# Issuing the sum-of-squares matmul behind the seventh contraction tile of a first phase

## The chip, the core and the metric

The kernel runs on one NeuronCore of a Trainium2 chip. The core has a matrix engine (PE, or TensorE), a vector engine (DVE), a scalar engine (ACT), GpSimd (POOL) and DMA queues; each engine works off its own list of instructions in the order in which they were put there, and waits on semaphores for what it needs from the others. The metric is the device time of one execution in microseconds (us).

## What is computed

A decoder trunk of four layers on one sequence of 256 tokens, model width 1024. Each layer is a macaron: a half-step SwiGLU feed-forward network (FFN), a token mixer (differential attention in layers 0 and 3, RWKV-7 in layer 1, sliding-window attention in layer 2), another half-step FFN. Each of these twelve sub-layers first normalises and modulates its input:

```
h = modulate(rms_norm(x, norm_g[i, 0]), sh1, sc1)      # x*rsqrt(mean(x*x)+eps)*g, then *(1+scale)+shift
x = x + 0.5 * g1 * swiglu(h, ffn_w_in[i, 0], ffn_w_out[i, 0])
...
def swiglu(h, w_in, w_out):
    gate, up = jnp.split(h @ w_in, 2, axis=-1)
    return (jax.nn.silu(gate) * up) @ w_out
```

## The kernel before, in words

The model width lies on the 128 partitions, in eight tiles x[0] to x[7] of 128x256 (tokens on the free axis). An fp32 product is made of three fp32r matmuls (`mm3`, lines 287 to 289): every operand is split in a high part hi and a low part lo, and hi·hi, hi·lo and lo·hi are summed. Weights are streamed from memory and split on chip as they come: hi on ACT (L269), lo on DVE (L271, 128x512, four to a slab). DVE also makes the adaLN vectors of the next sub-layers in halves of 128x1024 (`ada`, L350).

A sub-layer's **first phase** is made so that PE need not wait for the normalisation. While the sub-layer before ends, DVE adds each finished output tile to x (L589); then x·(g·(1+scale)), not yet divided by the root mean square, is split into `xh` (`pre`: hi on ACT, lo on DVE, L501). The factor 1/rms is one number per token, so it can be multiplied into the products afterwards: `unraw` (L547 to 554) does that on DVE (L553) on the way out of PSUM, with a shift term that ACT copies (`ub`, L552).

`first_units` (L530) issues the products of the first two or three weight units on `xh`: for each of the eight contraction tiles xh(0) to xh(7) nine matmuls (three output banks by `mm3`), then a fourth bank, then two more per further unit. Somewhere in between it calls `make`, which is `make_h` (L505). This does, in this order:

- `rstd` (L474): the matmul of the sum of squares, three fp32 instructions at L478, of the ones matrix with `ssum` (the squares of the first six tiles, summed up on POOL, L463) and with the last two squares `sq` (ACT, L455), into PSUM bank psc;
- the reciprocal root on DVE (`_rsqrt`): transposition of psc to `rsqt` (L410), ten small 128x8 operations (L419 to L435), transposition back to `rsq` (L441);
- for each of the eight tiles the scaled input: `xr` = x·a·rsq on DVE (L522), the high part of `h` on ACT (L524), the low part on DVE (L525).

The matmuls behind the first phase use `h`. In an FFN these are the up products of the second pair into psd, in the attention mixers products into psb. Their first `mm3` needs the high part of h(0), its second the low part.

This form of first phase stands at ten of the twelve sub-layers' starts. They are called B1 to B10 here, by the time of their sum-of-squares matmul in the profiled run: B1 219.4 us (into differential attention), B2 353.9 (out of it into an FFN), B3 548.5 (FFN into FFN), B4 1062.9 (RWKV into FFN), B5 1257.6 (FFN into FFN), B6 1451.6 (into sliding-window attention), B7 1545.5 (out of it into an FFN), B8 1739.6 (FFN into FFN), B9 1934.9 (into differential attention), B10 2071.0 (out of it into the last FFN). The program's very first FFN and RWKV use other code.

The order of instructions on each engine is not written out by hand. A scheduler fixes it when the kernel is built, from the dependences, the order in which the code issues the work, and its own costs; so a matmul that is issued later can change the order on DVE and ACT as well. At run time each engine keeps to its list.

Of the kernel before, what the change touches and what calls it, by code (L numbers as in the profile page):

```python
# [228 lines left out]
class Trunk:  # L229
# [300 lines left out]
    def first_units(self, w, make, tags):  # L530

        raw = bool(self.xh)
        hs = None if raw else make()
        banks = [self.ps(t) for t in tags for _ in range(2)]
        src, n = (self.xh, T + 2) if raw else (hs, T)
        self.xh = None
        order = [(k, (0, 1, 2)) for k in range(ND)] + [(k, (3,)) for k in range(ND)]
        order += [(k, (f,)) for f in range(4, 2 * len(w)) for k in range(ND)]
        for i, (k, fs) in enumerate(order):
            if raw and i == 4:  # L540
                hs = make()
            for f in fs:
                self.project(w[f // 2], 2, src, [banks[f // 2 * 2][:, :n], banks[f // 2 * 2 + 1][:, :n]], ks=(k,),
                             fs=(f % 2,), own=True)
        return banks, raw, hs
# [978 lines left out]
```

## Time and profile before

| what | value |
|---|---|
| median of 3 runs | 2263.47 us (2258.84, 2263.47, 2263.5) |
| profiled execution, its own time | 2263.52 us |
| span of it, first to last instruction | 2261.4 us |
| PE busy | 2173.4 us (96%) |
| DVE busy | 1761.5 us (78%) |
| ACT busy | 1191.8 us (53%) |
| POOL busy | 115.8 us (5%) |
| mean granted PE clock | 0.986 |

In the rows, each group's instructions are written as line, engine, operation, output<-inputs by the program's names. A row of a timeline begins with the start and the duration in us; where the engine stood idle before the instruction, the idle time and what ended it stand in brackets at the row's end. Durations overlap the next start a little, since the engines are pipelined; the spacing of starts is what an instruction costs its engine. The granted clock is a share of PE's full 2.4 GHz; 0.50 is its lower level, 1.2 GHz.

### The profile page before, as it was taken

Reading aid. Unit: us, or ns where it says so; the run is one execution under the profiler, and the core shown is the slowest. Engines: PE = TensorE matmul, PEld = TensorE weight load, DVE = VectorE, ACT = ScalarE, POOL = GpSimd, SP = SyncE. Lnnn points to the kernel's source line nnn. Section 1 sums busy time; section 2 is a strip of 40 time slices with the busy share of each in tenths; the row PEclk is TensorE's granted clock in tenths of the full one; section 3 lists DMA queues with packets and bytes.
Section 4 is the critical chain, followed back from the end, with each engine's and each line's share of the span. In section 5 each row is a group of like instructions: output and inputs, shape, how many; then the busy total and the mean of one; then the engine's idle time right before and its main releaser. Section 6 shows DMA issues by size and latency. Waiting matters only on the chain.

```text
span 2261.4 us, 47536 instructions
## 1 busy us (share of the span) xinstructions
PE 2173.4 (96%) x19230; PEld 2086.8 (92%) x19230; DVE 1761.5 (78%) x4005; ACT 1191.8 (53%) x2669; POOL 115.8 (5%) x213
## 2 busy tenths in 40 slices
PE   6999999999999898898999999999999999999999
PEld 6999898999999697677999999989999999989999
DVE  7887999889855776767988974779888965999554
ACT  3455766445444465445544644587445544767442
POOL 0001001001000400001000100101001000101000
PEclk9999999999999999889999999999999999999999
DMA  8885466887755410026788675446887765454552
GB/s 364 355 333 209 169 226 253 337 315 302 286 201 185 156 52 3 21 75 228 303 329 321 252 282 186 162 150 247 336 313 285 284 235 184 169 206 168 206 187 74
DMA packets 71356, 505.90 MB, mean 224 GB/s; under 512 B 7904, under 2 KB 9312, under 8 KB 10464
## 3 DMA queue, kind: packets, MB, share of 16 engines
q1 hardware_dynamic: 71136, 502.86, 58.6%
q8 instruction: 151, 2.47, 0.4%
q14 instruction: 69, 0.57, 0.1%
HBM read 501.78 MB, written 1.05 MB: 222 GB/s over the span
## 4 chain that ended last, share of the span: by engine, by line
PE 54%; DVE 7%; ACT 2%; issue 2%; POOL 0%; DVEq 0%; ACTq 0%; POOLq 0%
PE psa L289 5%; PE psa L288 5%; PE psa L287 5%; PE psd L288 4%; PE psd L289 4%; PE psd L287 4%; PE psb L287 4%; PE psb L288 4%; PE psb L289 4%; PE psc L287 3%; PE psc L288 3%; PE psc L289 3%; DVE lo L271 1%; DVE xh L501 1%; PE psc L1348 1%
## 5 line engine op out<-in xcount | busy, mean ns | idle before, releaser
L269 ACT CAST hi<-raw 128x512 fp32r<-128x512 f32 x1306 | 731.7, 618 | 706.7 <-issue 571.2
L271 DVE TENSOR_TENSOR lo<-raw,hi 128x512 fp32r<-128x512 f32 x1306 | 845.6, 690 | 232.3 <-ACT hi L269 230.6
L287 PE MATMUL psa<-h,hi 128*128 128x256 f32 x1336 | 375.7, 281 | 5.5 <-ACT h L561 5.5
L289 PE MATMUL psa<-h,lo 128*128 128x256 f32 x1336 | 377.7, 283 | 0.0
L288 PE MATMUL psa<-h,hi 128*128 128x256 f32 x1336 | 377.7, 283 | 0.0
L288 PE MATMUL psd<-h,hi 128*128 128x256 f32 x1256 | 355.4, 283 | 3.9 <-DVE h L525 3.9
L287 PE MATMUL psd<-h,hi 128*128 128x256 f32 x1256 | 353.7, 282 | 1.3 <-ACT ub L552 1.3
L289 PE MATMUL psd<-h,lo 128*128 128x256 f32 x1256 | 354.8, 282 | 0.0
L350 DVE SCALAR_TENSOR_TENSOR ada<-ada,cb 128x1024 f32<-128x1024 f32 x232 | 276.5, 1218 | 22.4 <-DMA ada<-in_ada_dram 22.2
L287 PEld LDWEIGHTS psa<-h,hi 128*128 128x128 f32 x1336 | 255.2, 191 | 6.2 <-ACT h L561 6.2
L288 PEld LDWEIGHTS psa<-h,hi 128*128 128x128 f32 x1336 | 252.9, 189 | 0.1
L289 PEld LDWEIGHTS psa<-h,lo 128*128 128x128 f32 x1336 | 252.6, 189 | 0.0
L288 PEld LDWEIGHTS psd<-h,hi 128*128 128x128 f32 x1256 | 236.8, 189 | 5.9 <-DVE h L525 5.1
L287 PEld LDWEIGHTS psd<-h,hi 128*128 128x128 f32 x1256 | 239.0, 190 | 2.5 <-ACT ub L552 1.7
L289 PEld LDWEIGHTS psd<-h,lo 128*128 128x128 f32 x1256 | 236.6, 188 | 0.3
L289 PE MATMUL psb<-g,lo 128*128 128x256 f32 x704 | 199.1, 283 | 0.0
L288 PE MATMUL psb<-g,hi 128*128 128x256 f32 x704 | 199.1, 283 | 0.0
L288 PE MATMUL psc<-g,hi 128*128 128x256 f32 x704 | 198.7, 283 | 0.0
L289 PE MATMUL psc<-g,lo 128*128 128x256 f32 x704 | 198.7, 283 | 0.0
L287 PE MATMUL psb<-g,hi 128*128 128x256 f32 x704 | 198.4, 283 | 0.0
L287 PE MATMUL psc<-g,hi 128*128 128x256 f32 x704 | 197.8, 282 | 0.0
L289 PEld LDWEIGHTS psb<-g,lo 128*128 128x128 f32 x704 | 135.3, 192 | 0.0
(379 smaller groups left out, 4449.0 us busy)
## 6 DMA issues: line engine op xcount, KB each, us to landing
raw<-in_ffi_dram SPq DMA_DIRECT2D x175, 1024.0 KB, 5.0
ada<-in_ada_dram SPq DMA_DIRECT2D x116, 1024.0 KB, 7.3
raw<-in_ffo_dram SPq DMA_DIRECT2D x88, 1024.0 KB, 4.9
raw<-in_ada_dram SPq DMA_DIRECT2D x24, 1024.0 KB, 4.9
raw<-in_daqk_dram SPq DMA_DIRECT2D x16, 1024.0 KB, 4.8
raw<-in_rwr_dram SPq DMA_DIRECT2D x12, 1024.0 KB, 4.8
raw<-in_ff_dram SPq DMA_DIRECT2D x8, 1024.0 KB, 11.3
raw<-in_dav_dram SPq DMA_DIRECT2D x8, 1024.0 KB, 4.8
```

The costliest lines, as they stand in the source:

```text
L269: nc.scalar.copy(hi[:, sl], raw[:, sl])
L271: eng.tensor_tensor(lo[:, sl], raw[:, sl], hi[:, sl].bitcast(F32), op=ALU.subtract)
L287: nc.tensor.matmul(out, whi, ahi, start=start, stop=False, skip_group_check=True)
L288: nc.tensor.matmul(out, whi, alo, start=False, stop=False, skip_group_check=True)
L289: nc.tensor.matmul(out, wlo, ahi, start=False, stop=stop, skip_group_check=True)
L350: nc.vector.scalar_tensor_tensor(wk, wk, 1.0, self.cond, op0=ALU.mult, op1=ALU.mult, accum_out=raw[:, k:k + 1])
L501: nc.vector.scalar_tensor_tensor(h[:, 1, :T], self.x[d], a[:, d:d + 1], h[:, 0, :T].bitcast(F32), op0=ALU.mult, op1=ALU.subtract)
L1348: nc.tensor.matmul(out, lhs(u)[hd[i]], rhs(u)[hd[i]], start=True, stop=True)
```

## The change

In `first_units`, `make` is called ahead of contraction tile 7 and no longer ahead of tile 4:

```diff
@@ first_units
         for i, (k, fs) in enumerate(order):
-            if raw and i == 4:
+            if raw and i == 7:
                 hs = make()
             for f in fs:
                 self.project(...)
```

On PE the three matmuls at L478 move behind three more contraction tiles, 27 matmuls. At B2, in the rows from the end of one contraction tile to the start of the next, before (psa, psd are the output banks, psc the bank of the sum of squares, hi and lo the split weights):

```order
L287 MATMUL psd_4415<-xh_4305,hi_4388 128x258
L288 MATMUL psd_4415<-xh_4305,hi_4388 128x258
L289 MATMUL psd_4415<-xh_4305,lo_4389 128x258
L478 MATMUL psc_4455<-ssum_4273,ones 128x256
L478 MATMUL psc_4455<-sq_4353,ones 128x256
L478 MATMUL psc_4455<-sq_4361,ones 128x256
L287 MATMUL psa_4413<-xh_4326,hi_4376 128x258
L288 MATMUL psa_4413<-xh_4326,hi_4376 128x258
```

and after the change:

```order
L287 MATMUL psd_4415<-xh_4355,hi_4388 128x258
L288 MATMUL psd_4415<-xh_4355,hi_4388 128x258
L289 MATMUL psd_4415<-xh_4355,lo_4389 128x258
L478 MATMUL psc_4482<-ssum_4273,ones 128x256
L478 MATMUL psc_4482<-sq_4353,ones 128x256
L478 MATMUL psc_4482<-sq_4361,ones 128x256
L287 MATMUL psa_4413<-xh_4363,hi_4376 128x258
L288 MATMUL psa_4413<-xh_4363,hi_4376 128x258
```

The three rows at psc stood between the tiles xh_4305 and xh_4326, the fourth and fifth; now they stand between xh_4355 and xh_4363, the seventh and eighth. It is the same at all ten places.

On DVE the scheduler fills in other work around the reciprocal root. At B2, from the last low part of xh (L501) on, before:

```order
L501 SCALAR_TENSOR_TENSOR xh_4363<-x_4359,mod_3218,xh_4363 128x256
L271 TENSOR_TENSOR lo_4646<-raw_4643,hi_4645 128x512
L410 STREAM_TRANSPOSE rsqt_4459<-psc_4455 128x256
L350 SCALAR_TENSOR_TENSOR ada_4830,modr_4832<-ada_4830,cb 128x1024
L419 TENSOR_SCALAR rm_4461<-rsqt_4459 128x8
L271 TENSOR_TENSOR lo_4658<-raw_4655,hi_4657 128x512
L426 TENSOR_SCALAR ry_4463<-rm_4461 128x8
L271 TENSOR_TENSOR lo_4658<-raw_4655,hi_4657 128x512
L428 TENSOR_TENSOR rz_4464<-ry_4463 128x8
L271 TENSOR_TENSOR lo_4658<-raw_4655,hi_4657 128x512
L429 TENSOR_TENSOR rz_4464<-rz_4464,rm_4461 128x8
L271 TENSOR_TENSOR lo_4658<-raw_4655,hi_4657 128x512
```

and after:

```order
L501 SCALAR_TENSOR_TENSOR xh_4363<-x_4359,mod_3218,xh_4363 128x256
L271 TENSOR_TENSOR lo_4646<-raw_4643,hi_4645 128x512
L350 SCALAR_TENSOR_TENSOR ada_4830,modr_4832<-ada_4830,cb 128x1024
L271 TENSOR_TENSOR lo_4658<-raw_4655,hi_4657 128x512 x3
L410 STREAM_TRANSPOSE rsqt_4486<-psc_4482 128x256
L271 TENSOR_TENSOR lo_4658<-raw_4655,hi_4657 128x512
L419 TENSOR_SCALAR rm_4488<-rsqt_4486 128x8
L350 SCALAR_TENSOR_TENSOR ada_4830,modr_4832<-ada_4830,cb 128x1024
L426 TENSOR_SCALAR ry_4490<-rm_4488 128x8
L271 TENSOR_TENSOR lo_4670<-raw_4667,hi_4669 128x512
L428 TENSOR_TENSOR rz_4491<-ry_4490 128x8
```

Ahead of the transposition at L410 there was one weight split (L271); now there are four and one ada half (L350). Further down at B2, ahead of the transposition back (L441) and of the first product that uses rsq (L553), before:

```order
L350 SCALAR_TENSOR_TENSOR ada_4830,modr_4832<-ada_4830,cb 128x1024
L435 SCALAR_TENSOR_TENSOR ry_4463<-rf_4465,ry_4463 128x8
L271 TENSOR_TENSOR lo_4797<-raw_4794,hi_4796 128x512
L441 STREAM_TRANSPOSE rsq_4475<-ry_4463 128x256
L271 TENSOR_TENSOR lo_4797<-raw_4794,hi_4796 128x512
L553 TENSOR_TENSOR sil_4399<-psa_4413,rsq_4475 128x256
```

and after:

```order
L271 TENSOR_TENSOR lo_4797<-raw_4794,hi_4796 128x512
L435 SCALAR_TENSOR_TENSOR ry_4490<-rf_4492,ry_4490 128x8
L350 SCALAR_TENSOR_TENSOR ada_4836,modr_4832<-ada_4836,cb 128x1024
L441 STREAM_TRANSPOSE rsq_4502<-ry_4490 128x256
L350 SCALAR_TENSOR_TENSOR ada_4836,modr_4832<-ada_4836,cb 128x1024
L553 TENSOR_TENSOR sil_4399<-psa_4413,rsq_4502 128x256
```

Two ada halves now stand there where one stood. At B5, which begins an FFN behind an FFN, from the last low part of xh on, before:

```order
L501 SCALAR_TENSOR_TENSOR xh_15460<-x_15456,mod_13995,xh_15460 128x256
L410 STREAM_TRANSPOSE rsqt_15557<-psc_15553 128x256
L271 TENSOR_TENSOR lo_15744<-raw_15741,hi_15743 128x512
L419 TENSOR_SCALAR rm_15559<-rsqt_15557 128x8
L350 SCALAR_TENSOR_TENSOR ada_16528,modr_15936<-ada_16528,cb 128x1024
L426 TENSOR_SCALAR ry_15561<-rm_15559 128x8
L271 TENSOR_TENSOR lo_15756<-raw_15753,hi_15755 128x512
```

and after:

```order
L501 SCALAR_TENSOR_TENSOR xh_15460<-x_15456,mod_13995,xh_15460 128x256
L271 TENSOR_TENSOR lo_15744<-raw_15741,hi_15743 128x512
L350 SCALAR_TENSOR_TENSOR ada_16729,modr_16725<-ada_16729,cb 128x1024
L271 TENSOR_TENSOR lo_15756<-raw_15753,hi_15755 128x512
L410 STREAM_TRANSPOSE rsqt_15584<-psc_15580 128x256
L271 TENSOR_TENSOR lo_15756<-raw_15753,hi_15755 128x512
L419 TENSOR_SCALAR rm_15586<-rsqt_15584 128x8
```

Two weight splits and an ada half have moved ahead of L410 there.

## Rows read from the trace of the kernel before

**Rows 1.** The page: busy time, share of the span and instructions of each engine.
```profile
PE 2173.4 (96%) x19230; PEld 2086.8 (92%) x19230; DVE 1761.5 (78%) x4005; ACT 1191.8 (53%) x2669; POOL 115.8 (5%) x213
```

**Rows 2.** Waits by engine and line: what waited, for what; total us, number of waits, the longest in us. PE's at the lines of the first phases and, in the second row, at an attention mixer's output; the last row is DVE's.
```profile
PE psc L478 <- POOL ssum L463: 8.1, 8, 2.0
...
PE psc L287 <- ACT o L561: 7.1, 3, 3.9
...
PE psd L288 <- DVE h L525: 3.9, 6, 0.9
...
PE psc L478 <- ACT sq L455: 0.8, 2, 0.6
...
DVE ada L350 <- DMA ada<-in_ada_dram: 22.2, 11, 4.0
```

**Rows 3.** PE's timeline at B2: two matmuls of the fourth contraction tile, the sum of squares, and PE's first two uses of h.
```profile
353.43 0.28 PE L287 MATMUL psd<-xh,hi 128*128 128x258 f32 x1
353.55 0.28 PE L288 MATMUL psd<-xh,hi 128*128 128x258 f32 x1
...
353.86 0.70 PE L478 MATMUL psc<-ssum,ones 128*128 128x256 f32 x2
...
369.48 0.39 PE L287 MATMUL psd<-h,hi 128*128 128x256 f32 x1 [0.74 <-ACT ub L552]
...
370.50 0.39 PE L288 MATMUL psd<-h,hi 128*128 128x256 f32 x1 [0.52 <-DVE h L525]
```

**Rows 4.** DVE's timeline at B2, from the transposition of the sum of squares to the first low parts of h. No row between them has an idle time in brackets.
```profile
357.00 0.44 DVE L410 STREAM_TRANSPOSE rsqt<-psc 128x256 f32<-128x256 f32 x1
357.37 1.18 DVE L350 SCALAR_TENSOR_TENSOR ada<-ada,cb 128x1024 f32<-128x1024 f32 x1
...
358.56 0.68 DVE L271 TENSOR_TENSOR lo<-raw,hi 128x512 fp32r<-128x512 f32 x1
359.16 0.16 DVE L426 TENSOR_SCALAR ry<-rm 128x8 int32<-128x8 int32 x1
...
368.07 1.65 DVE L522 SCALAR_TENSOR_TENSOR xr<-x,mod,rsq 128x256 f32<-128x256 f32 x4
369.65 0.41 DVE L553 TENSOR_TENSOR sil<-psb,rsq 128x256 f32<-128x256 f32 x1
369.98 1.65 DVE L525 SCALAR_TENSOR_TENSOR h<-xr,mod,h 128x256 fp32r<-128x256 f32 x4
```

**Rows 5.** PE's timeline at B5: the first row of the sum of squares, and the first use of the low part of h.
```profile
1257.56 0.70 PE L478 MATMUL psc<-ssum,ones 128*128 128x256 f32 x2 [2.02 <-POOL ssum L463]
...
1274.90 0.38 PE L288 MATMUL psd<-h,hi 128*128 128x256 f32 x1 [0.92 <-DVE h L525]
```

**Rows 6.** DVE's timeline at B5: the low part of xh(4), the transposition, and the last L553 ahead of the low part of h(0).
```profile
1256.45 0.47 DVE L501 SCALAR_TENSOR_TENSOR xh<-x,mod,xh 128x256 fp32r<-128x256 f32 x1
...
1261.34 0.45 DVE L410 STREAM_TRANSPOSE rsqt<-psc 128x256 f32<-128x256 f32 x1 [1.73 <-PE psc L478]
...
1274.03 0.42 DVE L553 TENSOR_TENSOR sil<-psb,rsq 128x256 f32<-128x256 f32 x1 [0.56 <-ACT ub L552]
```

**Rows 7.** Single rows of the timelines of DVE and PE at the other places: B3 and B8 (DVE's transposition), B7 (PE's first use of the low part of h).
```profile
550.98 0.45 DVE L410 STREAM_TRANSPOSE rsqt<-psc 128x256 f32<-128x256 f32 x1 [0.38 <-PE psc L478]
1743.66 0.45 DVE L410 STREAM_TRANSPOSE rsqt<-psc 128x256 f32<-128x256 f32 x1 [1.97 <-PE psc L478]
1561.59 0.38 PE L288 MATMUL psd<-h,hi 128*128 128x256 f32 x1 [0.42 <-DVE h L525]
```

**Rows 8.** The same at the three mixers and the last FFN: the first low part of h on DVE and PE's first matmul with h, at B1 (with the transposition ahead of them), B6, B9 and B10.
```profile
220.97 0.45 DVE L410 STREAM_TRANSPOSE rsqt<-psc 128x256 f32<-128x256 f32 x1 [1.03 <-PE psc L478]
231.37 0.88 DVE L525 SCALAR_TENSOR_TENSOR h<-xr,mod,h 128x256 fp32r<-128x256 f32 x2
231.70 0.36 PE L287 MATMUL psb<-h,hi 128*128 128x256 f32 x1
1460.15 0.49 DVE L525 SCALAR_TENSOR_TENSOR h<-xr,mod,h 128x256 fp32r<-128x256 f32 x1
1460.69 0.39 PE L288 MATMUL psb<-h,hi 128*128 128x256 f32 x1
1947.27 0.87 DVE L525 SCALAR_TENSOR_TENSOR h<-xr,mod,h 128x256 fp32r<-128x256 f32 x2
1950.09 0.36 PE L287 MATMUL psb<-h,hi 128*128 128x256 f32 x1
2084.14 1.66 DVE L525 SCALAR_TENSOR_TENSOR h<-xr,mod,h 128x256 fp32r<-128x256 f32 x4
2085.90 0.29 PE L287 MATMUL psd<-h,hi 128*128 128x256 f32 x1
```

**Rows 9.** Windows of 2 us: its length, then busy time and instructions of PE, PE's weight load, DVE, ACT and POOL, the clock granted to PE, the DMA share and GB/s. The first is behind the 3.9 us wait of rows 2, the second behind B3's sum-of-squares stall, the other three run from B5's.
```profile
345.00:347.00 2.00, 2.00 (x11) 2.00 (x11) 0.86 (x2) 0.38 (x2) 0.00 (x0) 0.51 0.41 164
549.00:551.00 2.00, 2.00 (x15) 1.87 (x14) 1.62 (x5) 1.03 (x3) 0.00 (x1) 1.00 0.03 8
1257.00:1259.00 2.00, 1.44 (x7) 1.39 (x8) 2.00 (x5) 1.59 (x5) 0.96 (x3) 0.83 0.02 8
1259.00:1261.00 2.00, 2.00 (x8) 1.73 (x7) 0.61 (x2) 0.09 (x1) 0.00 (x0) 0.50 0.00 0
1261.00:1263.00 2.00, 2.00 (x15) 1.91 (x15) 1.66 (x4) 0.60 (x2) 0.00 (x0) 0.81 0.00 0
```

## The prediction

> **What bounds the kernel now.** I read the page first: PE is busy 96% of the span, so whatever idles PE is time, and DVE's mean of 78% says little about a single stage [rows 1]. Then the table of waits: at the first phases PE waits in two places. It waits for the sum of squares, 8.1 us in eight waits for POOL's `ssum` and 0.8 us for ACT's squares, and further on for the scaled input, 3.9 us in six waits for the low part of `h` [rows 2]. The change goes for the first kind, 8.9 us in all. So the question is what the second kind does then, and for that I read the timelines of PE and DVE at each boundary.
>
> B2 shows the pattern. PE does the sum of squares at 353.86 without a wait, then the rest of the first phase at 0.12 us a matmul (353.43 to 353.55), and then stops twice, 0.74 and 0.52 us, until 370.50: for a bank that L553 must empty, and for the low part of h(0) [rows 3]. DVE is what it waits for. From the transposition at 357.00 to the low part of h(0) at 369.98 DVE has no gap at all [rows 4]: the reciprocal root takes so long only because weight splits and ada halves stand between its small operations. So PE's end of this stretch is set by what stands on DVE's list ahead of h(0), and not by when the sum of squares is done. B7 ends in the same way, with a wait of 0.42 us [rows 7], and B4 has B2's order on DVE.
>
> At B5 both kinds stand: PE stops at 1255.5 for 2.02 us, DVE later 1.73 us for the matmul and 0.56 us for ACT, and PE then still waits 0.92 us for h(0) [rows 5, 6]. B3 and B8 have the same order on DVE, with gaps ahead of the transposition of 0.38 and 1.97 us [rows 7].
>
> **The change, the matmul on PE.** No instruction is added or taken away in the phase; the three matmuls move by 27, that is 27 x 0.12 = 3.24 us later in PE's time [rows 3]. The stalls of 8.9 us at the sum of squares then mostly go, since `ssum` is done by then. At the FFN-to-FFN boundaries part comes back: at B5 the low part of xh(4) starts at 1256.45 and is ready by 1256.92, while PE has been through with xh(3) since 1255.5, so 1.4 of the 2.02 us would be spent waiting for xh(4) [rows 5, 6]. It does not matter for the sum, since PE reaches the first use of `h` early in any case and waits there. By itself, therefore, the removal is worth nothing wherever PE already ends in a wait for `h`: B2, B3, B4, B5, B7, B8, and B6 as good as.
>
> **The change, the list on DVE.** This carries the sum. The cost of one item is its spacing of starts at B2: a weight split 0.60 us (358.56 to 359.16), an ada half 1.19 us with its small follower (357.37 to 358.56), a product of the L522 kind 0.40 us (four from 368.07 to 369.65), L553 0.33 us (369.65 to 369.98) [rows 4]. I counted DVE's order of both kernels from the last low part of xh to that of h(0), and took as PE's loss the delay of h(0) less any slack it has.
> - B2 and B4: 11 splits and 2 ada halves become 13 and 4, and one more operation of 0.40 us (L664). 2 x 0.60 + 2 x 1.19 + 0.40 = 4.0 us each. Nothing hides it, since DVE has no gap there and PE is waiting already [rows 3, 4].
> - B3, B5, B8: 2 splits and 1 ada half more, one L553 and one L522 fewer: 1.20 + 1.19 - 0.33 - 0.40 = 1.67 us. This fills DVE's gaps, which are 1.73 + 0.56 us at B5 [rows 6] and about 0.7 and 2.3 us at B3 and B8 (the gap ahead of the transposition [rows 7], and 0.3 us at the ub copy, my estimate below B5's 0.56). Net +1.0, -0.6, -0.6 us.
> - B7: the same kind of exchange as B2, +3.8 us, with PE waiting already [rows 7].
> - B6: 3 splits ahead of h(0) and its followers become 9, and one ada half two; many small operations that stood bare now have cover. h(0) comes 4.3 us later and the last h 2.9 us; PE's use starts 0.1 us behind its arrival at 1460.6 [rows 8]. I take 3.0.
> - B1: DVE waits for the matmul here (1.03 us), and PE uses h(0) 0.3 us behind the start of its making [rows 8], so what the matmul loses goes through: 3.24 less the short stall ahead of it, and the last h only some 1.5 us late. Between 1.5 and 3.0, I take 2.4.
> - B9: h(0) 2.8 us later against a slack of 2.3 us (ready at about 1947.75, used at 1950.09) [rows 8]; the later ones have none. Between 0.5 and 2.8, I take 2.0. B10: 1.7 us later against a slack of 1.3 us [rows 8]: 0.4.
>
> Sum: 2.4 + 4.0 + 1.0 + 4.0 - 0.6 + 3.0 + 3.8 - 0.6 + 2.0 + 0.4 = **+19.4 us**. The work pulled ahead is not extra work; DVE has it behind it later. But no wait of PE for weight splits stands among its large waits [rows 2], so nothing is given back.
>
> **The clock.** The waits for `h` grow by the delay and by the stall that went. At B2, B4 and B7 they become about 5 us long, at B3 and B6 3.5 to 4, at B1 and B9 some 2.4, at B5 and B8 about 2. In the trace, the granted clock behind an idle PE of 3.9 us is 0.51, its lower level [rows 2, 9]. Behind B5's stall of 2.02 us it falls to 0.50 too, but behind B3's stall of the same length it stays at 1.00 [rows 9], so at 2 us it is open. A fall costs (1 - 0.83 + 1 - 0.50 + 1 - 0.81) x 2 us = 1.7 us of full-speed work [rows 9]. B5 and B8 exchange a fall at the sum of squares for one at `h`. Five new falls for the long waits and some 1.3 for the two of 2.4 us make 6.3 x 1.7 = 10.7 us at most; the h tiles behind the first are paced by DVE, which hides a little of a slow PE. I take 1.4 each, **+8.8 us**; the lower end is nothing.
>
> Together 2263.5 + 19.4 + 8.8 = 2291.7, about **2292 us**. The profiled run's 2263.52 us is the median of the runs.
>
> **The rivals.**
> Faster: the stall removed pays. If `h` arrived at least as early as PE, the 8.9 us and the two clock falls of B5 and B8 (3.4 us) would go, to 2251 us. This holds where DVE's gaps are at least as long as what is put ahead of h(0). That is so at B5 and B8 alone, and PE's six waits for `h` speak against it elsewhere [rows 2]. Chance 0.08. The Trainium skill, Perfetto Trace Analysis, section Optimization Strategy, advises to find the gaps of the engine one optimises for and to make what it waits for start sooner; with PE the busiest, closing the gap at L478 would be worth the gap. No run here shows that yet, and the same section says that the most contended engine may change over a kernel, which is what the gapless DVE of B2 shows.
>
> No change: DVE's delay is half-covered and the 8.9 us cancels it, 2259 to 2268 us. It would need PE to have some 10 us of slack at the h uses, and only B9 and B10 have any [rows 8]. Chance 0.07.
>
> Slower with the clock unmoved: only the lists count, 2263.5 + 19.4 = 2283 us. For it speaks B3's stall [rows 9]. Chance 0.22.
>
> Slower still: the ada halves pulled ahead of the root wait for their transfer. DVE waits for ada transfers 11 times in the trace, up to 4.0 us [rows 2]; at B2, B4 and B7 such a wait would now hold back the whole chain, 12 us more, to 2304 us. Chance 0.10.
>
> That the change does not do what it says is excluded: the matmul moves at all ten places.
>
> **How the numbers follow.** The forecast has 0.53. The range of 2270 to 2306 us reaches from a sum of lists that is too large by two thirds without the clock to the late transfers; it leaves out the two cases at and below the old time and a little at each end, some 0.2. A measurement here can tell 0.2% from no change, 4.5 us. Faster 0.09, same 0.06, slower 0.85.
>
> **What would show it.** In the changed kernel the waits of L478 for `ssum` should be near nothing, and the waits of psd and psb for `h` and `ub` should grow from 3.9 us for psd's `h` to 20 or more in all, with single ones of about 5 us at B2, B4 and B7. DVE should have no gap ahead of the transposition at B3, B5 and B8. The two-microsecond windows behind the long waits should show a clock near 0.5. I am wrong if DVE's spacing in these stretches gets shorter, if PE's waits for `h` stay below 1 us, or if the growth sits at other lines.

## The result

The changed kernel takes 2285.98 us (median of 4 runs, 2284.4 to 2291.37), the kernel before 2261.53 us (4 runs, 2258.84 to 2263.5): 24.5 us more, a ratio of 1.011 with a 95% interval of 1.009 to 1.0129. The prediction was 2292 us, range 2270 to 2306. The profiled run of the changed kernel took 2285.21 us, its span is 2283.1 us.

PE's waits in the profile of the changed kernel, at the lines of rows 2:

```profile
PE psd L287 <- ACT ub L552: 20.9, 7, 5.2
...
PE psa L288 <- DVE xh L501: 3.9, 5, 1.0
PE psa L788 <- DVE qk L553: 3.4, 1, 3.4
PE psb L287 <- ACT h L524: 2.5, 3, 1.5
...
PE psd L288 <- DVE h L525: 1.3, 3, 0.5
PE psb L288 <- DVE h L525: 1.2, 3, 0.5
```

The wait of L478 for `ssum`, 8.1 us in [rows 2], has no row any more. In its place PE waits 20.9 us at the FFNs' first matmul with `h` (the first row). The kernel before has there

```profile
PE psd L287 <- ACT ub L552: 1.3, 2, 0.7
```

Besides, PE waits 5.0 us in all for `h` in the mixers and for its low part (rows 4 to 6; 4.6 us before), and 3.9 us for `xh` (0.9 us before). The profile puts the first row down to `ub`, but that is only the copy that ACT ended last. ACT's timeline at B2 in the changed kernel:

```profile
373.17 0.49 ACT L524 ACTIVATE h<-xr,mod 128x256 fp32r<-128x256 f32 x1
373.57 0.14 ACT L552 COPY ub<-psb 128x1 f32<-128x1 f32 x1
```

The matmul writes to psd and reads the high part of h(0), which is done at 373.66, 0.06 us ahead of its start at 373.72. That copy of `ub` is taken from another bank, psb, and DVE had read psd for the last time by 372.38. The matmul starts about 0.05 us behind the high part at all seven FFNs. So by the code and these times PE waits for h(0) itself; it does so at B2 of the kernel before too (high part done at 369.43, matmul at 369.48), and not, as the prediction has it, for a bank that L553 must empty. DVE's timeline at B2 shows why h(0) is late; the rows answer to [rows 4]:

```profile
357.14 0.68 DVE L271 TENSOR_TENSOR lo<-raw,hi 128x512 fp32r<-128x512 f32 x1
357.74 1.21 DVE L350 SCALAR_TENSOR_TENSOR ada<-ada,cb 128x1024 f32<-128x1024 f32 x1
...
358.89 1.88 DVE L271 TENSOR_TENSOR lo<-raw,hi 128x512 fp32r<-128x512 f32 x3
360.69 0.43 DVE L410 STREAM_TRANSPOSE rsqt<-psc 128x256 f32<-128x256 f32 x1
...
368.35 1.22 DVE L350 SCALAR_TENSOR_TENSOR ada<-ada,cb 128x1024 f32<-128x1024 f32 x1
...
369.86 1.18 DVE L350 SCALAR_TENSOR_TENSOR ada<-ada,cb 128x1024 f32<-128x1024 f32 x1
...
373.88 0.47 DVE L664 SCALAR_TENSOR_TENSOR gf<-gf,ub,sil 128x256 f32<-128x256 f32 x1
...
374.61 0.47 DVE L525 SCALAR_TENSOR_TENSOR h<-xr,mod,h 128x256 fp32r<-128x256 f32 x1
```

DVE is never idle here either; it does the pulled-ahead splits and ada halves, and the first low part of `h` starts at 374.61 where it stood at 369.98. PE's timeline beside it, answering to [rows 3], and the windows behind the wait (columns as in [rows 9]):

```profile
373.72 0.58 PE L287 MATMUL psd<-h,hi 128*128 128x256 f32 x1 [4.55 <-ACT ub L552]
...
375.14 0.58 PE L288 MATMUL psd<-h,hi 128*128 128x256 f32 x1 [0.41 <-DVE h L525]
```

```profile
374.00:376.00 2.00, 1.58 (x7) 1.29 (x8) 2.00 (x6) 2.00 (x7) 0.00 (x0) 0.50 1.00 422
376.00:378.00 2.00, 2.00 (x11) 2.00 (x11) 2.00 (x6) 1.69 (x5) 0.00 (x0) 0.50 0.27 115
...
570.00:572.00 2.00, 1.24 (x9) 1.14 (x10) 2.00 (x6) 2.00 (x7) 0.00 (x0) 1.00 0.92 389
572.00:574.00 2.00, 2.00 (x19) 2.00 (x18) 2.00 (x6) 2.00 (x6) 0.00 (x0) 1.00 0.15 57
...
1278.00:1280.00 2.00, 1.82 (x13) 1.73 (x14) 2.00 (x6) 2.00 (x7) 0.00 (x0) 1.00 0.77 324
...
1775.00:1777.00 2.00, 2.00 (x12) 2.00 (x11) 2.00 (x6) 1.99 (x5) 0.00 (x0) 0.50 0.04 12
...
1470.00:1472.00 2.00, 2.00 (x8) 1.78 (x8) 1.47 (x4) 1.96 (x6) 0.00 (x0) 0.50 0.00 0
...
1578.00:1580.00 2.00, 2.00 (x10) 2.00 (x11) 2.00 (x7) 1.45 (x5) 0.00 (x0) 0.50 1.01 426
```

The wait grew from 1.26 us (0.74 + 0.52) to 4.96, and PE then runs at half its clock: 11 matmuls in 2 us, where 19 run at full clock from 572 to 574, behind B3's wait. The windows stand, in their order, for B2 (two), B3 (two), B5, B8, B6 and B7.

To place the loss I cut each profile at PE's first matmul on `xh` of each boundary, and at the end of B3's FFN. The tables give, against the profile of before, by how much the low part of h(0) starts later, counted from that first matmul, and by how much the whole segment up to the next boundary grew, in us.

| changed kernel | B1 | B2 | B3 | B4 | B5 | B6 | B7 | B8 | B9 | B10 |
|---|---|---|---|---|---|---|---|---|---|---|
| h(0) later by | 0.8 | 3.7 | 1.1 | 3.6 | -1.1 | 5.2 | 4.2 | -0.5 | 3.0 | 1.5 |
| segment longer by | 0.4 | 5.0 | 0.9 | 4.3 | -1.2 | 8.4 | 5.2 | 0.6 | 3.5 | 0.3 |

The segments, with 0.5 us ahead of B1, sum up to 27.9 us. The profiled run is only 21.7 us longer than that of before (2285.21 - 2263.52), since the RWKV mixer between B3 and B4, whose first phase the change does not touch, took 6.3 us less. That is chance, as the last section shows. Where e3 to e6 leave a boundary as it was, its segment comes back within 0.9 us at B1 to B4, B6, B7 and B10, but is off by up to 2.1 us at B5, 1.6 at B8 and 2.5 at B9, where the lower clock comes in one execution and not in another. So the entries of B5, B8 and B9 are good to some 2 us only.

### The profile page after: what moved, and what is told of

It reads as the page before. It is cut to its first block, busy times and chain, and to the rows that moved or that the text cites. A ratio compares the mean times of both kernels' runs of the same rounds, so it can differ in the third digit from the quotient of the medians.

```text
span 2283.1 us, 47594 instructions
## 1 busy us (share of the span) xinstructions
PE 2178.9 (95%) x19230; PEld 2091.2 (92%) x19230; DVE 1761.9 (77%) x4005; ACT 1192.1 (52%) x2669; POOL 118.9 (5%) x213
## 4 chain that ended last, share of the span: by engine, by line
PE 52%; DVE 8%; ACT 3%; issue 2%; DVEq 0%; ACTq 0%
PE psa L288 5%; PE psa L289 5%; PE psa L287 4%; PE psd L288 4%; PE psd L289 4%; PE psd L287 4%; PE psb L287 4%; PE psb L288 4%; PE psb L289 3%; PE psc L287 3%; PE psc L288 3%; PE psc L289 3%; DVE lo L271 2%; DVE xh L501 1%; ACT hi L269 1%
## 5 line engine op out<-in xcount | busy, mean ns | idle before, releaser
L271 DVE TENSOR_TENSOR lo<-raw,hi 128x512 fp32r<-128x512 f32 x1306 | 846.5, 691 | 237.6 <-ACT hi L269 237.0
L287 PE MATMUL psd<-h,hi 128*128 128x256 f32 x1256 | 356.3, 284 | 20.9 <-ACT ub L552 20.9
L350 DVE SCALAR_TENSOR_TENSOR ada<-ada,cb 128x1024 f32<-128x1024 f32 x232 | 276.0, 1219 | 18.8 <-DMA ada<-in_ada_dram 18.6
L287 PEld LDWEIGHTS psd<-h,hi 128*128 128x128 f32 x1256 | 241.5, 192 | 22.7 <-ACT ub L552 22.4
L288 PEld LDWEIGHTS psd<-h,hi 128*128 128x128 f32 x1256 | 239.4, 191 | 3.4 <-DVE h L525 2.3
```

What stands on the lines that cost most here:

```text
L271: eng.tensor_tensor(lo[:, sl], raw[:, sl], hi[:, sl].bitcast(F32), op=ALU.subtract)
L287: nc.tensor.matmul(out, whi, ahi, start=start, stop=False, skip_group_check=True)
L288: nc.tensor.matmul(out, whi, alo, start=False, stop=False, skip_group_check=True)
L350: nc.vector.scalar_tensor_tensor(wk, wk, 1.0, self.cond, op0=ALU.mult, op1=ALU.mult, accum_out=raw[:, k:k + 1])
```

## The experiments

The theory: PE's loss at a boundary is the delay of h(0) on DVE, less any slack, and some clock; the place of the sum of squares on PE counts only through DVE's list. The main rival: the late matmul itself is the loss. Medians are compared with runs of the kernel before on the same chip, 2259.76 us (17 runs) for e1 to e4, 2259.45 (13) for e5 to e8, 2259.60 (17) for e9 to e12.

**e1 and e2: one tile and two tiles later.**

```diff
-            if raw and i == 4:
+            if raw and i == 5:      # e1; 6 in e2
```

> The sum of squares one contraction tile later instead of three. Theory (the lists on DVE count, not the place of the matmul): counted from the order on DVE, h(0) comes 0.6 us later at B2 and B4, 0.4 at B7, 1.2 at B6, and not later at B3, B5, B8, B9, B10; the waits stay short, so the clock falls nowhere new. Sum +2 to +4 us over the kernel before. Rival (the loss goes with how far the matmul moves on PE): a third of the 24 us, +8 us.

> The sum of squares two contraction tiles later. Theory: h(0) later by 1.3 us at B2 and B4, 1.0 at B7, 1.2 at B6, by 1.2 at B3, B5 and B8 of which DVE's gaps there take all but 0.5 at B3; few or no falls of the clock. Sum +5 to +8 us. Rival (distance on PE): two thirds of the 24 us, +16 us.

e1: 2263.12 us, ratio 1.0013 (0.9999 to 1.0026), +3.4 us. e2: 2268.73 us, ratio 1.0036 (1.0023 to 1.0049), +9.0 us. The theory's +2 to +4 holds (the interval reaches from -0.2 to +5.9 us, so e1 is not clear of no change), its +5 to +8 is a little short, and the rival's +8 and +16 are out: one tile, two and three cost 3.4, 9.0 and 24.5 us, which is not proportional to the distance.

e1 shows the clock apart from the delay. At B2 its h(0) comes no later at all, and yet the segment is 1.3 us longer. PE's two waits there and the clock behind them:

```profile
370.48 0.39 PE L287 MATMUL psd<-h,hi 128*128 128x256 f32 x1 [1.19 <-ACT ub L552]
371.50 0.38 PE L288 MATMUL psd<-h,hi 128*128 128x256 f32 x1 [0.52 <-DVE h L525]
```

```profile
372.00:374.00 2.00, 2.00 (x15) 2.00 (x14) 2.00 (x6) 2.00 (x7) 0.00 (x0) 0.67 0.05 20
374.00:376.00 2.00, 2.00 (x11) 2.00 (x11) 2.00 (x6) 2.00 (x6) 0.00 (x0) 0.50 0.00 0
```

Waits of 1.71 us in all were followed by the lower clock; the kernel before, with 1.26 us at the same place, shows no fall there.

**e3, e5, e6: the change at some of the boundaries only**, the others at the fourth tile.

```diff
-            if raw and i == 4:
+            if raw and i == self.at:
...
+                        self.at = 7 if s == 2 else 4      # e3: B2, B4, B7, B10
+                        self.at = 7 if s == 0 else 4      # e5: B3, B5, B8
+            self.at = 7      # e6, in the attention mixers: B1, B6, B9; 4 in the FFNs
```

> The changed place only where an FFN follows a mixer (B2, B4, B7, B10); the other six as before. The order on DVE there is that of the changed kernel, elsewhere that of the kernel before. Theory: the loss of these four places alone, by the changed kernel's trace 5.0 + 4.3 + 5.2 + 0.4, +15 us. Rival (every place loses about the same): four tenths of 24 us, +10 us. If most of the loss were in the mixers: under +5 us.

> The changed place only where an FFN follows an FFN (B3, B5, B8). Theory: DVE's gaps there take in what is pulled ahead, +0.9 - 1.2 + 0.6 by the changed kernel's trace, so between -2 and +3 us over the kernel before, although 6 us of stalls at the sum of squares go. Rival (every place loses the same): three tenths of 24 us, +7 us. Rival (a stall removed pays): -6 us.

> The changed place only at the three attention mixers (B1, B6, B9). Theory: +0.4 + 8.4 + 3.5 by the changed kernel's trace, +10 to +13 us, most of it at B6. The prediction's own terms for these places, 2.4 + 3.0 + 2.0 and some clock, would give +9. Rival (equal shares): +7 us.

e3: 2273.84 us, 1.0066 (1.005 to 1.0082), +14.1. e5: 2262.84 us, 1.002 (1.001 to 1.003), +3.4. e6: 2269.02 us, 1.0046 (1.003 to 1.0062), +9.6. Together 27.1 us for the change's 24.5. The four FFNs behind a mixer carry half of it, the three mixers a third, and the three boundaries with the long stalls at the sum of squares an eighth. e5 is just above what was expected: the stalls it removes are not paid out at all.

**e4: the delay alone, with nothing moved on PE.**

```diff
+            if floor is None and self.slow:
+                g.tensor_reduce(m, first.unsqueeze(2).to_broadcast([P, nk, 480]), op=ALU.max, axis=AX.X)
+                g.tensor_scalar(m, m, scale, eps, op0=ALU.mult, op1=ALU.add)
```

> The sum of squares stays at the fourth tile at all ten places; at B2, B4, B7 and B10 one operation of some 4.0 us is put into the reciprocal root on DVE (a maximum over 480 copies of the same eight values), and the scheduler takes a little other work out of the way. Nothing is moved on PE. Theory (delay of h(0) on DVE is PE's loss): 4.0 + 4.0 + 3.4 + 5, and 1 to 1.5 us of clock at three or four of them, +17 to +22 us. Rival (the loss needs the late matmul, DVE has room): under +5 us.

2284.30 us, 1.0104 (1.0084 to 1.0125), +24.5 us: more than expected. That it is as much as the change costs is a coincidence, since the change loses next to nothing at B10 and a third in the mixers; what counts is the place by place below. The group of the inserted operation in DVE's lines:

```profile
L419 DVE TENSOR_REDUCE rm<-rsqt 128x8 f32<-128x3840 f32 x4 | 16.6, 4142 | 0.0
```

At its four places h(0) came 3.9, 4.5, 3.6 and 6.6 us later and the segments were 5.2, 5.8, 5.7 and 6.6 us longer. At B2, B4 and B7 that is the change's loss (5.0, 4.3 and 5.2 us) or more. So a delay made on DVE alone is a loss on PE of that size and up to 2 us on top.

**e7 and e8: splits taken off DVE**, with the sum of squares at the fourth and at the seventh tile.

```diff
-                    wg, wu = (self.load(A["ffi"][(base + j) * 2 + f]) for f in range(2))
+                    wg, wu = (self.load(A["ffi"][(base + j) * 2 + f], pool=j == 1 and (l, s) != self.plan[0]) for f in range(2))
```

> The kernel before, with the weight splits of each FFN's second pair (eight of 128x512, save the first FFN's) made on GpSimd and no longer on DVE. Theory: by the order, DVE's list ahead of h(0) is shorter by 1.4 us at B2, 2.1 at B4, 3 to 5 at B3, B5, B7, B8; PE's waits for h and ub (some 5 us in all) go, the stalls at the sum of squares stay: -3 to -5 us, if GpSimd is done in time. GpSimd's 128x256 addition takes 0.9 us, so eight splits take some 15 us, an estimate; where they come too late PE waits for weights instead, up to +5 us at each FFN. Rival (DVE's list is not what PE waits for): no change.

> The changed kernel (the sum of squares behind the seventh tile at all ten places) with the same splits on GpSimd. Theory: DVE's list ahead of h(0) is about as long as in the kernel before or shorter (B2 15.1 us for 14.9, B4 14.2 for 14.9, B7 15.2 for 14.5, B3, B5, B8 some 3 us shorter), so the losses into the FFNs go and only those of the mixers stay, some 12 us: 2265 to 2272 us, 14 to 20 under the changed kernel. Rival (the late matmul itself is the loss): still about 2285 us. GpSimd too late: above 2285 us, with waits of PE for lo.

e7: 2292.0 us, 1.0145 (1.0128 to 1.0162), +32.6 us. e8: 2321.59 us, 1.0274 (1.0257 to 1.0291), +62.1 us. Both expectations failed, and not by GpSimd being late: PE has no wait for its splits. DVE's timeline of e8 at B2:

```profile
355.76 1.21 DVE L350 SCALAR_TENSOR_TENSOR ada<-ada,cb 128x1024 f32<-128x1024 f32 x1
...
356.90 2.29 DVE L350 SCALAR_TENSOR_TENSOR ada<-ada,cb 128x1024 f32<-128x1024 f32 x1
...
363.59 1.25 DVE L419 TENSOR_SCALAR rm<-rsqt 128x8 f32<-128x8 f32 x1
...
369.49 0.68 DVE L271 TENSOR_TENSOR lo<-raw,hi 128x512 fp32r<-128x512 f32 x1
370.09 0.15 DVE L429 TENSOR_TENSOR rz<-rz,rm 128x8 f32<-128x8 f32 x1
```

and GpSimd's beside it:

```profile
356.03 6.55 POOL L271 TENSOR_TENSOR lo<-raw,hi 128x512 fp32r<-128x512 f32 x3
363.31 6.24 POOL L271 TENSOR_TENSOR lo<-raw,hi 128x512 fp32r<-128x512 f32 x4 [0.73 <-ACT hi L269]
```

While GpSimd splits, until 369.55, DVE's ada half takes 2.29 us instead of 1.21 and its 128x8 operation 1.25 instead of 0.15. So the shorter list took longer: h(0) came 6.6, 6.1 and 7.9 us later at B2, B4 and B7, and the segments grew by 8.3, 8.5 and 9.8. In e7 the split also stood ahead of the additions of `ssum` on GpSimd, and L478's wait for it rose from 8.1 to 17.0 us. The experiments do not take the suspected cost away, as meant; they confirm the link from h(0) to the loss, with another cause of delay.

**e9 and e10: a shorter root.** One refinement step of the reciprocal root is left out, at the fourth and the seventh tile.

```diff
+        if not self.short:
             g.tensor_tensor(z, y, y, op=ALU.mult)
             g.tensor_tensor(z, z, m, op=ALU.mult)
             g.tensor_scalar(f, z, -0.1875 / 16, 0.625 / 4, op0=ALU.mult, op1=ALU.add)
             g.tensor_tensor(f, f, z, op=ALU.mult)
             g.scalar_tensor_tensor(y, f, -0.9375, y, op0=ALU.add, op1=ALU.mult)
+        else:
+            g.tensor_scalar(y, y, -0.5, None, op0=ALU.mult)
```

(The five lines under the `if` are the old ones, only indented.) These kernels leave out part of the computation and are no replacement for the kernel before.

> The sum of squares at the fourth tile as before; the reciprocal root has one refinement step and not two, four small operations fewer (part of the computation is left out: the root is less exact). By the order on DVE, with each operation that goes a weight split between two of them goes behind h(0) as well: h(0) comes 4.4 us earlier at B2, 3.6 at B4, 3.7 at B7, 2.7 at B3, B5, B8. Theory: PE's waits for h and ub, some 5 us in all, go; the stalls at the sum of squares stay: -3 to -6 us. Rival (DVE's list is not what sets PE's wait): -0.5 us or less.

> The changed kernel with the same short root (the second refinement step is left out). By the order h(0) comes at B2, B4 and B7 about when it does in the kernel before (14.6 us behind the next to last xh for 14.9, 14.9 and 14.5), and at B3, B5, B8 2 to 4 us earlier with DVE's gaps gone. Theory: the loss into the FFNs goes, what is left is B6 and B9, and the gain at B3, B5, B8 shows at last: -4 to +3 us against the kernel before, 22 to 28 under the changed kernel. Rival (the late matmul is the loss whatever DVE does): about +22 us.

e9: 2243.43 us, 0.9924 (0.9911 to 0.9938), -16.2 us. e10: 2260.86 us, 1.0009 (0.9996 to 1.0022), +1.3 us. e10 decides between theory and rival: with the matmul as late as in the changed kernel, but h(0) at B2, B4 and B7 at -0.9, -0.6 and +0.7 us against the kernel before, these segments differ from it by -0.9, -0.6 and +2.0 us. The 24 us of the change are not in the late matmul. The place still matters with the short root (e10 less e9 is 17.4 us). h(0) is again later, by 2.6, 2.4 and 4.3 us at B2, B4 and B7, but these segments grow by only 0.5, 0.6 and 2.9 us, since PE does not wait for h in e9 and so has slack to lose. Most of it lies in the mixers B1, B6 and B9, where h(0) is later by 2.3, 3.1 and 7.4 us and the segments are longer by 3.7, 3.5 and 3.7. In e9 PE's waits for h and ub have no row left, while the stalls at the sum of squares stand as before:

```profile
PE psc L483 <- POOL ssum L468: 8.1, 8, 2.0
PE psc L483 <- ACT sq L460: 1.1, 3, 0.6
```

(The shift of lines is the edit's.) So the gain of 16 us is had with these stalls in place. I had expected -3 to -6, the waits alone. Missed were the clock falls of B5 and B8, which e9 does not have behind the same stalls (their segments are 3.3 and 2.8 us shorter, against waits of some 0.9 and 0.8), and 3.8 us in the mixers B1, B6 and B9. That the short root is what kept the clock up is not shown: e3 and e4 have no fall behind B5's stall either, with the old root.

**e11 and e12: the root on GpSimd**, in full.

```diff
-        g = nc.vector
+        g = nc.gpsimd if self.onpool else nc.vector
...
-        g.scalar_tensor_tensor(y, z, -3.0, y, op0=ALU.add, op1=ALU.mult)
+            g.tensor_scalar(z, z, -3.0, None, op0=ALU.add)
+            g.tensor_tensor(y, z, y, op=ALU.mult)
```

> The sum of squares at the fourth tile; the whole reciprocal root between the two transpositions (twelve small operations) on GpSimd, full exactness. A GpSimd operation of 128x4 takes 0.40 to 0.48 us in the traces, so the root takes 5 to 6 us, an estimate, for 8.4 us on DVE with its splits in between. Theory: h(0) 2 to 3 us earlier at B2, B3, B4, B5, B7, B8, PE's waits there go: -3 to -6 us, less if DVE's splits, which now stand idle behind the root, become late for PE. Rival: no change, or slower, where GpSimd's work slows DVE's operations beside it as with the splits on GpSimd.

> The changed place with the root on GpSimd. Theory: h(0) about when it came in the kernel before at B2, B4 and B7, earlier at B3, B5, B8; with the stalls at the sum of squares gone: -3 to +5 us against the kernel before, some 20 to 28 under the changed kernel, and B6 and B9 as what is left of the loss. Rival (the late matmul itself): +22 us.

e11: 2272.98 us, 1.0053 (1.0041 to 1.0065), +13.4 us; e12: 2275.45 us, 1.0072 (1.006 to 1.0084), +15.9 us. Both missed on the slow side. h(0) came 3.8 to 6.5 us earlier into the FFNs in e11, as the theory wanted, but DVE now stands in front of its list until GpSimd is through (a wait of DVE), and PE runs into splits that were made late (waits of PE), in e11:

```profile
DVE rsq L449 <- POOL ry L441: 33.5, 11, 3.5
```

```profile
PE psd L289 <- DVE lo L271: 4.9, 3, 1.8
PE psc L289 <- DVE lo L271: 1.2, 2, 0.6
```

Of the 12.2 us that e11's segments are longer, the RWKV mixer aside, 12.0 sit in the three mixers (3.3, 3.7 and 5.0 us); what holds them up there was not followed further. This is read as the bound of the theory, that an earlier h(0) pays only as long as DVE does not idle for it; it is argued and not shown. The place costs only 2.5 us more here (e12 less e11), and the two sets of five runs overlap (2268.84 to 2275.27, 2273.76 to 2279.57).

A version as exact as the kernel before that beats it was not found.

## Why the prediction was right

- **DVE's list sets PE's end.** Right: e4 makes the change's loss at B2, B4 and B7 without the change, e10 has the change nearly without its loss there. The reading of one wait was wrong, as said above: at the FFNs PE waits for the high part of h(0) and not for a bank. The sum does not hang on it, since L553 and h(0) stand on the same list of DVE.
- **The stalls removed are worth nothing by themselves.** Right: 8.9 us of stalls went, and e5, where 6 of them lie, is 3.4 us slower. Part came back as waits for xh, 3.9 us for 0.9, as worked out for B5 (1.0 us there, where the prediction has 1.4).
- **B2, B4, B7: 4.0, 4.0, 3.8 us.** h(0) came 3.7, 3.6 and 4.2 us later. **B3, B5, B8: +1.0, -0.6, -0.6.** Measured 1.1, -1.1, -0.5. The signs at B5 and B8 come from the one execution that was read. There the clock fell behind the stall at the sum of squares ([rows 9] for B5), so h(0) came 23.8 and 23.3 us behind the first matmul on xh, and 21.7 at B3. In e3's profile, where B5 is as before, it comes at 21.7 there too, behind the same stall without a fall: PE's stall, DVE's gap ahead of the transposition and the window behind (lines are shifted by one) are

```profile
1263.21 0.70 PE L477 MATMUL psc<-ssum,ones 128*128 128x256 f32 x2 [2.01 <-POOL ssum L462]
1265.65 0.45 DVE L409 STREAM_TRANSPOSE rsqt<-psc 128x256 f32<-128x256 f32 x1 [0.39 <-PE psc L477]
1265.00:1267.00 2.00, 2.00 (x17) 1.95 (x16) 1.61 (x5) 0.29 (x1) 0.00 (x0) 1.00 0.00 0
```

  In the changed kernel it is 22.7 or 22.8 at all three. So the gaps of 1.73 and 1.97 us that the prediction let DVE fill came with the slow clock of that execution. Without a fall they are 0.39 us at B5 and, in e4's and e6's profiles, at B8, like B3's 0.38, and the change costs each of the three about 1.0 us. Three times that would be e5's +3.4 us, an estimate; how often the fall comes is not known.
- **B10: 0.4.** The segment grew by 0.3.
- **B6: 3.0 us, measured 8.4.** The term was mis-sized by its first reader of the root. I looked at h(0) alone (4.3 us counted, 5.2 measured) and took less because of the later ones; but PE stops ahead of it already, for the q and k products that L553 scales. PE's timeline at B6 in the changed kernel:

```profile
1466.82 0.67 PE L788 MATMUL psa<-msk 128*128 128x384 bf16 x2 [3.42 <-DVE qk L553]
1469.02 0.79 PE L287 MATMUL psb<-h,hi 128*128 128x256 f32 x2 [1.53 <-ACT h L524]
```

  The two waits of 4.95 us and the half clock behind them make most of the 8.4.
- **B1: 2.4 us, measured 0.4.** A step was wrong: the matmul does not move by 27 there. In PE's list of the kernel before it stands behind 60 matmuls on xh already, since the scheduler had moved it, and behind 72 in the changed kernel; at the other nine places it goes from 36 (37 to 43 for its later instructions at some) to 63. The statement ahead of the prediction that all ten places are alike is wrong in this. h(0) came 0.8 us later.
- **B9: 2.0 us, measured 3.5**, near by luck. h(0) came 3.0 us later (2.8 counted), but PE had made that up by the segment's 450th matmul, which starts 64.4 us into it in both profiles. The loss arises at the mixer's other end, where PE waits for its output `o`, first in the kernel before, then in the changed one:

```profile
2061.73 0.50 PE L287 MATMUL psc<-o,hi 128*128 128x256 f32 x2 [2.39 <-ACT o L561]
2081.19 0.80 PE L287 MATMUL psc<-o,hi 128*128 128x256 f32 x2 [4.45 <-ACT o L561]
```

  Behind it PE runs at half clock (11 matmuls from 2083 to 2085 at 0.50, for 18 from 2062 to 2064 at 1.00 before). e6, which changes B9, has the same wait of 4.44 us and 3.4 us on the segment; e3 and e5, which do not, have 2.39 us. So the new order reaches 130 us beyond the place, and the prediction has no term for it; what holds `o` up was not followed.
- **The clock: 8.8 us.** Where the segment grew by more than h(0) came later, the surplus is 1.3 us at B2, 0.7 at B4, 3.2 at B6, 1.0 at B7 and 1.1 at B8: 7.3 us, which holds the falls and the later tiles together. Falls show behind the waits of B2, B4, B6, B7 and B8; B3's wait was 2.4 us and not 3.5 to 4, and had none. The waits of some 2.4 us at B1 and B9 did not come (0.9 and 1.1 us, in pieces), nor did a fall behind them. Which wait brings a fall stays open: B3, B5 and B8 have the same wait of 2.37 us, and B8 alone fell.
- Summed: 28.2 us forecast, 27.9 in the segments, 24.5 between the medians. So close a sum is luck: B6 took 5.4 us more than its term and B9 1.5, B1 2.0 less, and falls were counted at B1, B3 and B9 that did not come there. The mechanism holds at the FFNs; the growth in the mixers sits in good part at lines that the prediction does not name (3.4 us at L788, 2.1 at `o`).

## What to carry to other kernels

A matmul that waits is worth moving only if what comes out of it is not what the engine waits for next; look for the next wait on the same chain and ask which engine's list feeds it. When a scheduler fixes the order, moving one instruction on one engine rewrites the lists of the others: count what now stands ahead of the critical operation there, at every place, and well beyond it (B9), and check that the instruction itself moved as far as the code says. Shortening the in-order chain (four small operations fewer gave 16 us, at the price of exactness) was worth more than any place tried for the matmul. A stretch that was read in one execution may hold a fall of the clock that the next one lacks: compare like places (B3 with B5 and B8) before taking a gap as given.

## What the runs showed that I had not expected

The RWKV mixer, whose code no experiment but the roots changes, took 1.8 to 7.9 us less in each of the thirteen later profiles than in the profile of before. The windows of 20 us, first of the kernel before, then of the changed kernel, show the clock in it:

```profile
980.00:1000.00 20.00, 18.86 (x223) 15.10 (x219) 9.65 (x26) 7.82 (x23) 0.00 (x0) 0.57 0.15 54
```

```profile
986.00:1006.00 20.00, 19.06 (x337) 15.87 (x337) 13.12 (x42) 9.44 (x30) 0.00 (x0) 0.91 0.30 107
```

The same stretch ran at 0.57 of the clock in one execution and at 0.91 in another. Runs of the kernel before spread from 2253 to 2266 us; differences of two single profiles here are good to some 5 us, and segments have to be compared instead. And GpSimd's splits slow DVE's operations beside them: 2.29 us for 1.21, and 1.25 us for 0.15. The price was about 1.1 us on either, whatever its size. The Trainium skill, Perfetto Trace Analysis, section Optimizing Scalar/DVE Operations, has it that GpSimd and DVE share an SBUF read port, so that offloading between the two might not help. These rows agree with it; the port itself shows in no row.
